# The small inverses and the layer norm of a hybrid attention block, issued step by step by the emission order

## The chip, the cores and the metric

One Trainium2 chip; the kernel runs on one of its cores. The metric is the device time of one execution in microseconds (us). Engines are named as in the profile: PE (TensorE's matmuls), PEld (its weight loads), DVE (VectorE), ACT (ScalarE), POOL (GpSimd), and SP (SyncE, which only issues DMAs here).

## The reference

One post-norm residual layer over x of 2048 tokens by 1024 channels, all float32. One wide projection of x feeds two token mixers: branch A, a gated delta rule with 4 heads of 128, and branch B, a sliding-window attention with a sink logit. Their outputs are gated, projected back to 1024 channels, merged, projected once more, and normalised. What the change touches is the triangular inverse inside the delta rule and the layer norm at the end:

```python
lower = jnp.where(strict, jnp.einsum("bnhid,bnhjd->bnhij", k_beta, k) * decay, 0.0)
t_inv = lax.linalg.triangular_solve(eye + lower, eye, left_side=True, lower=True, unit_diagonal=True)
...
r = DEEPNORM_ALPHA * x + out
mu = jnp.mean(r, axis=-1, keepdims=True)
var = jnp.mean(jnp.square(r - mu), axis=-1, keepdims=True)
y = (r - mu) * lax.rsqrt(var + LN_EPS) * ln_g + ln_b
```

## The kernel before

The 2048 tokens go in four chunks of T = 512. Every large product is made of three matmuls (high x high, high x low, low x high; lines 175 to 177), so PE has far more columns to stream than any other engine has elements. The order of PE's instructions is that of the program text (`manual_schedule` for PE). The other engines' and SP's instructions are put in order when the program is built, by a list scheduler that looks at when each is ready and, among ready ones, takes the one that was emitted first.

The text's own order comes from a small planner, `Order`. Its clock `st.now` counts PE time as the kernel's constants estimate it: 216 ns for a 512-column product (`PE_R`). "Dense" work (the large projections) is emitted piece by piece in the order of the string `ORDER`; after each piece `run` emits the next step of every task whose due time has come. A task is a generator that yields (PE time of the step, delay until its next step). `until(name)` polls every 500 ns until another task has ended; `finish(name)` moves the clock on until it has.

In chunks 1 to 3 the order begins

```python
ORDER = "kv k0 k1 q0 v0 p p p q1 p g w0 v1 z0 k2 q2 v2 g g g k3 z1 g q3 g w1 v3 g g g g z2 g g g z3 g g g"
```

`p` is a quarter of the output projection of the chunk before; after the fourth, `layer_norm` of that chunk is emitted in one go. `g` is a gate projection, `w0` the queries of the first half of the attention, which then spawns the task `attend` (window0).

Each of the 4 heads of a chunk passes through these tasks: `front` (k by k products at line 389, the matrix m2, its diagonal blocks of 32 to `scr_m` in DRAM and back as `su`), `inverse` (`small_inverse`: lines 905 to 917 on DVE, a chain of 16 pairs of a product, line 916, and a sum, line 917; then `xi` goes to `scr_p`, line 425), `levels` (loads it as `p_`, line 437; first matmuls at line 449), `back` (four rounds of PE line 496, DVE `bt` 498, PE 501, DVE `wc` 503, PE 507, DVE `S` 508) and `delta_gate`. `inverse` is spawned LAT_M = 4.4 us after its transfers are issued and emitted whole; `levels` and `back` are due LAT_INV = 29.6 us after the products of line 389, and `levels` yields LAT_D = 5.4 us between its loads and its first matmuls.

The layer norm before: for each of four blocks of 128 tokens, two bn_stats on DVE (line 699), the factors (line 685 to 691, with a power on POOL, line 851), and the normalising pass r*rs + nm on ACT (line 701); then for four quarters of the channels a load of gain and bias (`lg`, a buffer of the pool tag "s") and on POOL, in two halves each, a product (line 708) and a sum (line 709); then two output DMAs (line 712). The result lives in the buffers `yBh` and `yBl`, which `attend` of the same stretch overwrites from line 634 on.

Of the kernel before, what the change touches and what calls it, by code (L numbers as in the profile page):

```python
# [8 lines left out]
F32 = mybir.dt.float32  # L9
F32R = mybir.dt.float32r  # L10
AF = mybir.ActivationFunctionType
ALU = mybir.AluOpType
# [4 lines left out]
P = 128  # L17
# [3 lines left out]
NB = T // P  # L21
# [36 lines left out]
def view(t, off, dims):  # L58
    return bass.AP(tensor=t.tensor, offset=t.offset + off, ap=[list(t.ap[0])] + dims)


def build(tc, xt, xn, wk, wg, par, lnp, cst, out, seq=2048):
    nc = tc.nc
    NCH = seq // T
    with ExitStack() as ctx:
# [355 lines left out]
            yield 4 * PE_F, 0  # L421

        def inverse(h, su, xi):
            small_inverse(tc, pt.tile([P, 256], F32, name="xt"), su, xi.rearrange("p (c i) -> p c i", i=32))
            nc.sync.dma_start(out=at(scr_p[h % 2], 0, [[P, P], [1, P]]), in_=xi)
            yield 0, 0

        def levels(c, h, m2, q_):

            yield from st.until(f"front{h}")  # L430
            if h:
                yield from st.until(f"levels{h - 1}")
            p_ = pt.tile([P, NB, 64], F32, name="p_")
            nc.gpsimd.memset(p_[:32, :, 32:], 0.0)
            nc.gpsimd.memset(q_, 0.0)
            for i in range(4):
                nc.sync.dma_start(out=p_[32 * i:32 * i + 32, :, 32 * (i % 2):32 * (i % 2) + 32],
                                  in_=at(scr_p[h % 2], 1024 * i, [[32, 32], [4096, NB], [1, 32]]))
            yield 0, LAT_D
            for i in range(4):  # L440
                bi = slice(32 * i, 32 * i + 32)
                tc.keep_in_program_order(nc.vector.transpose(q_[bi, :, bi], p_[bi, :, 32 * (i % 2):32 * (i % 2) + 32]))
            copy = (lambda o, i: nc.scalar.activation(o, i, AF.Copy), nc.vector.tensor_copy)
            lo, hi = [slice(64 * s, 64 * s + 32) for s in range(2)], [slice(64 * s + 32, 64 * s + 64) for s in range(2)]
            x_ = pt.tile([P, NB, 64], F32, name="x_")
            ps = [p4(), pp.tile([P, NB, P], F32, name="pp")]
            for b in range(NB):
                for s in range(2):
                    nc.tensor.matmul(ps[s][hi[s], b, :32], m2[lo[s], b, hi[s]], p_[lo[s], b, :32], start=True, stop=True)
            for s in range(2):  # L450
                copy[s](x_[hi[s], :, :32], ps[s][hi[s], :, :32])
            yield 8 * PE_Q, LAT_B
            ps = [p4(), pp.tile([P, NB, P], F32, name="pp")]
            for b in range(NB):
                for s in range(2):
                    nc.tensor.matmul(ps[s][lo[s], b, :32], x_[hi[s], b, :32], q_[hi[s], b, hi[s]], start=True, stop=True)
            for b in range(NB):
                nc.tensor.matmul(ps[0][hi[0], b, :32], q_[hi[0], b, hi[0]], x_[hi[0], b, :32], start=True, stop=True)
            copy[0](p_[hi[0], :, :32], ps[0][hi[0], :, :32])
            for s in range(2):  # L460
                copy[1 - s](q_[lo[s], :, hi[s]], ps[s][lo[s], :, :32])
            yield 12 * PE_Q, LAT_B
            ps = p4()
            for b in range(NB):
                nc.tensor.matmul(ps[64:, b, :64], m2[:64, b, 64:], p_[:64, b], start=True, stop=True)
            copy[0](x_[64:], ps[64:, :, :64])
            yield 4 * PE_T, LAT_B
            ps = p4()
            for b in range(NB):
                nc.tensor.matmul(ps[:64, b, :64], x_[64:, b], q_[64:, b, 64:], start=True, stop=True)  # L470
            copy[1](q_[:64, :, 64:], ps[:64, :, :64])
            yield 4 * PE_T, LAT_B
# [100 lines left out]
        def attend(c, gp):  # L573
            for b0 in (0, 2):
                yield from st.until(f"qT{b0}")
            if not gp:
                c.yBh = py.tile([P, 4, T], F32R, name="yBh")
                c.yBl = py.tile([P, 4, T], F32R, name="yBl")
            zb = [c.z[f"zb{2 * gp + g}"] for g in range(2)]
# [100 lines left out]
            for bp in range(2):  # L680
                nc.vector.scalar_tensor_tensor(c.ra[bp][:, :, es], xr[bp], 2.0 * ALPHA, pss[bp], ALU.mult, ALU.add)

        def norm_factors(c, bst):
            mv = sm.tile([P, 2], F32, name="mv")
            nc.vector.bn_aggr(mv, bst)
            va = sm.tile([P, 1], F32, name="va")
            nc.vector.tensor_scalar(va, mv[:, 1:2], 4.0e-5, None, ALU.add)
            rs = sm.tile([P, 1], F32, name="rs")
            rsqrt(nc, sm, rs, va, mhalf)
            nm = sm.tile([P, 1], F32, name="lnm")  # L690
            nc.vector.scalar_tensor_tensor(nm, mv[:, 0:1], -1.0, rs, ALU.mult, ALU.mult)
            return rs, nm

        def layer_norm(c):
            for b in range(NB):
                r = c.ra[b // 2][:, b % 2]
                bst = sm.tile([P, 4, 6], F32, name="st", bufs=1)[:, :2]
                for i in range(2):
                    nc.vector.bn_stats(bst[:, i], r[:, 512 * i:512 * i + 512])
                rs, nm = norm_factors(c, bst)  # L700
                nc.scalar.activation(r, r, AF.Identity, scale=rs, bias=nm)
            for eg in range(4):
                es = slice(256 * eg, 256 * eg + 256)
                lg = pa.tile([P, 2, 256], F32, name="s")
                nc.sync.dma_start(out=lg, in_=bass.AP(tensor=lnp.tensor, offset=lnp.offset + 256 * eg, ap=[[0, P], [D, 2], [1, 256]]))
                for bp in range(2):
                    r = c.ra[bp][:, :, es]
                    nc.gpsimd.tensor_tensor(r, r, lg[:, 0:1].to_broadcast([P, 2, 256]), ALU.mult)
                    nc.gpsimd.tensor_tensor(r, r, lg[:, 1:2].to_broadcast([P, 2, 256]), ALU.add)
            for bp in range(2):  # L710
                t0 = c.i * T + bp * 256
                nc.sync.dma_start(out=out[t0:t0 + 256].rearrange("(b p) e -> p b e", p=P), in_=c.ra[bp])
# [47 lines left out]
        def piece(c, w):  # L760
            if w == "start":
                st.dense([start(c)])
            elif w == "kv":
                st.dense([window_kv(c)])
            elif w == "g":
                st.dense([gate(c, next(c.gates))])
            elif w == "p":
                e = next(c.projects)
                st.dense([project(c.prev, e)])
                if e == 3:  # L770
                    layer_norm(c.prev)
            elif w[0] == "w":
                st.dense([window_q(c, int(w[1]))])
            elif w[0] == "z":
                st.dense([silu2(c, f"h{w[1]}3")])
            else:
                st.dense([head_in(c, int(w[1]), w[0])])

        st = Order()
# [26 lines left out]
class Order:  # L806

    def __init__(self):  # L810
        self.now, self.tasks, self.done = 0.0, [], set()

# [4 lines left out]
    def step(self, t):  # L817
        try:
            dur, lat = next(t[2])
        except StopIteration:  # L820
            self.done.add(t[1])
            self.tasks.remove(t)
            return
        self.now += dur
        t[0] = self.now + lat
# [22 lines left out]
def rsqrt(nc, sm, r, a, mhalf):  # L848

    n = a.shape[1]  # L850
    nc.gpsimd.tensor_tensor(r, a, mhalf[:, :n], ALU.pow)
    t = sm.tile([P, n], F32, name=f"rsq{n}")
    nc.vector.tensor_tensor(t, r, r, ALU.mult)
    nc.vector.scalar_tensor_tensor(t, t, -0.5, a, ALU.mult, ALU.mult)
    nc.vector.scalar_tensor_tensor(r, t, 1.5, r, ALU.add, ALU.mult)
# [43 lines left out]
def small_inverse(tc, t, su, xi):  # L899


    rows = su.rearrange("p (m r k) -> p m r k", r=2, k=32)
    tm = t.rearrange("p (m k) -> p m k", k=32)
    nc = tc.nc
    tc.keep_in_program_order(nc.vector.memset(view(su, 33, [[66, 16]]), 0.0))
    for m in range(0, 16, 8):
        ms = slice(m, m + 8)
        nc.vector.tensor_tensor(tm, rows[:, ms, 1], view(su, 66 * m + 1, [[66, 8], [0, 32]]), ALU.mult)
        nc.vector.tensor_tensor(rows[:, ms, 0], rows[:, ms, 0], tm, ALU.add)
    nc.vector.memset(view(su, 0, [[33, 32]]), 1.0)  # L910
    tx = t.rearrange("p (c r k) -> p c r k", r=2, k=32)
    for i in range(30, -1, -2):
        n = 32 - i
        u = view(su, 33 * i, [[0, 4], [32, 2], [1, n]])
        x = view(xi, i, [[32, 4], [0, 2], [1, n]])
        nc.vector.tensor_tensor(tx[:, :, :, :n], u, x, ALU.mult)  # L916
        nc.vector.tensor_reduce(xi[:, :, i:i + 2], tx[:, :, :, :n], AX.X, ALU.add)  # L917


def tables(seq):  # L920
# [71 lines left out]
```

## Time and profile before

| | |
|---|---|
| median of 3 runs | 1720.17 us (1720.06 to 1723.12) |
| the profiled execution | 1723.25 us, span of its instructions 1721.5 us |
| PE busy | 1631.3 us, 95% of the span |
| DVE busy | 1020.2 us, 59% |
| ACT busy | 547.8 us, 32% |
| POOL busy | 374.2 us, 22% |
| mean granted TensorE clock | 0.983 |

Busy times of different engines overlap; only what keeps PE idle, or its clock low, can be won without taking work from PE.

### The profile page before, as it was taken

The page shows a single profiled execution, that of the slowest core. Times are in us where ns is not written, and L with a number is a line of the kernel's source. Part 1 is how long each engine was busy: PE and PEld are TensorE (multiplying, and loading weights), DVE is VectorE, ACT ScalarE, POOL GpSimd, SP SyncE. Part 2 cuts the span into 40 slices and gives each one's busy share as a digit, 9 for nine tenths or more (in the row PEclk, how much of TensorE's full clock was granted, in tenths as well). Part 3 has the DMA queues.
Part 4 walks back from the last instruction along what each step waited for, and adds up shares of the span by engine and source line. Part 5 has one row for each costly group of instructions (what it writes and reads, how often), then busy time and mean ns, then how long its engine had stood idle before and what let it go on. Part 6 is the DMA issues. An engine that isn't in the chain of part 4 may idle for free.

```text
span 1721.5 us, 27328 instructions
## 1 busy us (share of the span) xinstructions
PE 1631.3 (95%) x9846; PEld 1372.2 (80%) x9846; DVE 1020.2 (59%) x3118; ACT 547.8 (32%) x1496; POOL 374.2 (22%) x366
## 2 busy tenths in 40 slices
PE   8989999999897999999989899999998989999997
PEld 6867878778886878888888687888888868888787
DVE  5677678446757756435546765643554867463245
ACT  3454445333232532321303243323130334333100
POOL 4543454341334111010003311100010521100002
PEclk9999999999999999999999999999999999999999
DMA  8765675667685455557555645556656554464862
GB/s 301 241 219 193 209 245 190 216 204 237 204 251 186 130 168 167 142 165 240 176 167 172 205 133 159 159 152 191 190 167 213 176 168 142 145 189 141 279 204 80
DMA packets 189159, 323.39 MB, mean 188 GB/s; under 512 B 31072, under 2 KB 45408, under 8 KB 188896
## 3 DMA queue, kind: packets, MB, share of 16 engines
q1 hardware_dynamic: 185184, 316.40, 58.3%
q0 software_dynamic: 3840, 5.25, 1.4%
q8 instruction: 78, 1.28, 0.3%
q14 instruction: 57, 0.47, 0.1%
HBM read 244.97 MB, written 71.37 MB: 184 GB/s over the span
## 4 chain that ended last, share of the span: by engine, by line
PE 71%; DVE 13%; DMA 9%; issue 3%; ACT 2%; SPq 1%; POOL 1%; ACTq 0%; DVEq 0%; POOLq 0%
PE mm L175 19%; PE mm L177 18%; PE mm L176 18%; DVE xt L916 2%; DMA wb<-kw_o 2%; PE pp L627 2%; DVE kr L867 2%; PE pp L619 1%; DVE xi L917 1%; DMA w<-in_wg 1%; DMA su<-scrm 1%; DMA wb<-kw_kv 1%; PE pp L588 1%; PE pp L589 1%; PE pd L501 1%
## 5 line engine op out<-in xcount | busy, mean ns | idle before, releaser
L175 PE MATMUL mm<-xh,wb 128*128 128x512 f32 x1128 | 474.4, 421 | 0.9 <-DMA wb<-kw_h 0.9
L177 PE MATMUL mm<-xh,wb 128*128 128x512 f32 x1128 | 447.1, 396 | 0.0
L176 PE MATMUL mm<-xl,wb 128*128 128x512 f32 x1128 | 446.2, 396 | 0.0
L177 PEld LDWEIGHTS mm<-xh,wb 128*128 128x128 f32 x1128 | 213.5, 189 | 50.2
L175 PEld LDWEIGHTS mm<-xh,wb 128*128 128x128 f32 x1128 | 214.6, 190 | 44.6 <-issue 5.7
L176 PEld LDWEIGHTS mm<-xl,wb 128*128 128x128 f32 x1128 | 215.2, 191 | 35.6
L157 POOL TENSOR_TENSOR wb<-w,wb 128x512 fp32r<-128x512 f32 (+1 forms) x110 | 149.7, 1362 | 193.2 <-ACT wb L156 171.2
L175 PE MATMUL mm<-wb,s 128*128 128x256 f32 x384 | 113.2, 295 | 18.7 <-DMA wb<-kw_o 12.9
L175 PE MATMUL mm<-wb,xh 128*128 128x256 f32 (+1 forms) x384 | 115.1, 300 | 11.0 <-DVE rope L866 4.2
L176 PE MATMUL mm<-wb,s 128*128 128x256 f32 x384 | 109.9, 286 | 1.0 <-POOL wb L157 1.0
L176 PE MATMUL mm<-wb,xh 128*128 128x256 f32 (+1 forms) x384 | 110.1, 287 | 0.3 <-POOL wb L157 0.3
L177 PE MATMUL mm<-wb,s 128*128 128x256 f32 x384 | 109.7, 286 | 0.0
L177 PE MATMUL mm<-wb,xl 128*128 128x256 f32 (+1 forms) x384 | 109.6, 285 | 0.0
L156 ACT ACTIVATE wb<-w 128x512 fp32r<-128x512 f32 (+1 forms) x110 | 68.8, 629 | 115.8 <-PE mm L177 55.7
L916 DVE TENSOR_TENSOR xt<-su,xi 128x16 f32<-128x16 f32 (+15 forms) x256 | 99.4, 388 | 5.5
L175 PEld LDWEIGHTS mm<-wb,s 128*128 128x128 f32 x384 | 74.4, 194 | 22.9 <-DMA wb<-kw_o 15.4
L605 ACT ACTIVATE s<-s,nm 128x256 f32<-128x256 f32 (+1 forms) x128 | 62.7, 491 | 82.6 <-DVE nm L599 82.6
L175 PEld LDWEIGHTS mm<-wb,xh 128*128 128x128 f32 x384 | 74.0, 193 | 14.3 <-issue 6.3
L917 DVE TENSOR_REDUCE xi<-xt 128x8 f32<-128x16 f32 (+15 forms) x256 | 74.6, 291 | 5.9
L176 PEld LDWEIGHTS mm<-wb,s 128*128 128x128 f32 x384 | 74.3, 194 | 1.6 <-POOL wb L157 1.5
L176 PEld LDWEIGHTS mm<-wb,xh 128*128 128x128 f32 x384 | 74.0, 193 | 0.9 <-POOL wb L157 0.6
L177 PEld LDWEIGHTS mm<-wb,s 128*128 128x128 f32 x384 | 74.2, 193 | 0.0
(666 smaller groups left out, 3165.4 us busy)
## 6 DMA issues: line engine op xcount, KB each, us to landing
wb<-kw_h SPq DMA_DIRECT2D x96, 512.0 KB, 4.1
wb<-kw_g SPq DMA_DIRECT2D x96, 512.0 KB, 4.0
w<-in_wg SPq DMA_DIRECT2D x106, 256.0 KB, 4.1
wb<-kw_b SPq DMA_DIRECT2D x48, 512.0 KB, 4.6
wb<-kw_o SPq DMA_DIRECT2D x36, 512.0 KB, 4.9
kw_h<-wb SPq DMA_DIRECT2D x32, 512.0 KB, 3.9
kw_g<-wb SPq DMA_DIRECT2D x32, 512.0 KB, 3.4
wb<-kw_q SPq DMA_DIRECT2D x24, 512.0 KB, 4.0
```

The lines of the kernel that those rows point to most:

```text
L156: nc.scalar.activation(hi, raw, AF.Copy)
L157: nc.gpsimd.tensor_tensor(lo, raw, hi.bitcast(F32), ALU.subtract)
L175: nc.tensor.matmul(ps, sh, mh, start=(first and i == 0), stop=False)
L176: nc.tensor.matmul(ps, sh, ml, start=False, stop=False)
L177: nc.tensor.matmul(ps, sl, mh, start=False, stop=(last and i == n))
L501: nc.tensor.matmul(ps, q_[:, b], bt, start=True, stop=True)
L588: nc.tensor.matmul(psc[v][:, g, k0:], c.qT[v][:, b, g], kT[v][:, ks], start=True, stop=False)
L605: nc.scalar.activation(s[:, g, k0:], s[:, g, k0:], AF.Exp, bias=nm[:, g:g + 1], scale=0.125, accum_out=su[:, g:g + 1])
L627: nc.tensor.matmul(psY[64 * v:64 * v + 64], c.vs[b + kb][:, 64 * v:64 * v + 64], pTs[v][:, kb], start=(kb == kbs[0]), stop=(kb == 1))
L867: nc.vector.tensor_tensor(d[:, :, 0:8], a[:, 0, :, 0], a[:, 1, :, 1], ALU.subtract)
L916: nc.vector.tensor_tensor(tx[:, :, :, :n], u, x, ALU.mult)
L917: nc.vector.tensor_reduce(xi[:, :, i:i + 2], tx[:, :, :, :n], AX.X, ALU.add)
```

## The change

`inverse` and `layer_norm` become tasks that emit a step at a time. A step yields `None` in place of a PE time: the planner's clock then stands still and the task's own due time moves on. `small_inverse` yields after each of its two halves of row updates (1.8 us) and after each of its 16 pairs (420 + 40 n ns, n = 2 to 32 even). `layer_norm` is spawned after the fourth `p`; it yields 2.5 us after the factors of each of four blocks and 1.8 us after each of 16 steps. The normalising pass, the gain and the bias are now two DVE instructions for each 128 tokens by 256 channels: (r - mu) * gain, then r * rs + bias; ACT's pass and POOL's products and sums are gone. `levels` waits for the end of `inverse`, and `attend` of window0 for the end of `norm`. In `norm_factors`, `mv` and `rs` get four buffers.

```diff
         def inverse(h, su, xi):
-            small_inverse(tc, pt.tile([P, 256], F32, name="xt"), su, xi.rearrange("p (c i) -> p c i", i=32))
+            yield from small_inverse(tc, pt.tile([P, 256], F32, name="xt"), su, xi.rearrange("p (c i) -> p c i", i=32))
             nc.sync.dma_start(out=at(scr_p[h % 2], 0, [[P, P], [1, P]]), in_=xi)
-            yield 0, 0
+            yield None, 0
 
         def levels(c, h, m2, q_):
...
             if h:
                 yield from st.until(f"levels{h - 1}")
+            yield from st.until(f"inverse{h}")
...
             if not gp:
+                if c.i:
+                    yield from st.until("norm")
                 c.yBh = py.tile([P, 4, T], F32R, name="yBh")
...
-        def norm_factors(c, bst):
-            mv = sm.tile([P, 2], F32, name="mv")
+        def norm_factors(c, bst, bufs=None):
+            mv = sm.tile([P, 2], F32, name="mv", bufs=NB)
...
-            rs = sm.tile([P, 1], F32, name="rs")
+            rs = sm.tile([P, 1], F32, name="rs", bufs=NB)
             rsqrt(nc, sm, rs, va, mhalf)
+            if bufs:
+                return rs, mv[:, 0:1]
...
         def layer_norm(c):
+            fs = []
             for b in range(NB):
...
-                rs, nm = norm_factors(c, bst)
-                nc.scalar.activation(r, r, AF.Identity, scale=rs, bias=nm)
+                rs, mu = norm_factors(c, bst, NB)
+                fs.append((r, rs, mu))
+                yield None, 2500
             for eg in range(4):
...
-                for bp in range(2):
-                    r = c.ra[bp][:, :, es]
-                    nc.gpsimd.tensor_tensor(r, r, lg[:, 0:1].to_broadcast([P, 2, 256]), ALU.mult)
-                    nc.gpsimd.tensor_tensor(r, r, lg[:, 1:2].to_broadcast([P, 2, 256]), ALU.add)
+                for r, rs, mu in fs:
+                    nc.vector.scalar_tensor_tensor(r[:, es], r[:, es], mu, lg[:, 0], ALU.subtract, ALU.mult)
+                    nc.vector.scalar_tensor_tensor(r[:, es], r[:, es], rs, lg[:, 1], ALU.mult, ALU.add)
+                    yield None, 1800
...
                 if e == 3:
-                    layer_norm(c.prev)
+                    st.spawn("norm", layer_norm(c.prev), 0)
...
     def step(self, t):
...
+            return
+        if dur is None:
+            t[0] += lat
             return
...
 def small_inverse(tc, t, su, xi):
...
         nc.vector.tensor_tensor(rows[:, ms, 0], rows[:, ms, 0], tm, ALU.add)
+        yield None, 1800
...
         nc.vector.tensor_reduce(xi[:, :, i:i + 2], tx[:, :, :, :n], AX.X, ALU.add)
+        yield None, 420 + 40 * n
```

## Rows read from the trace of the kernel before

**Rows 1.** The page, part 1: busy us (share of the span) xinstructions of each engine.

```profile
PE 1631.3 (95%) x9846; PEld 1372.2 (80%) x9846; DVE 1020.2 (59%) x3118; ACT 547.8 (32%) x1496; POOL 374.2 (22%) x366
```

**Rows 2.** Windows: length, busy us of PE, PEld, DVE, ACT, POOL; PEclk; DMA.

```profile
500.00:560.00 60.00, 50.31 (x336) 42.80 (x333) 48.89 (x139) 15.68 (x41) 25.58 (x27) 0.97 0.63 193
920.00:980.00 60.00, 51.24 (x337) 44.28 (x337) 46.64 (x129) 13.91 (x32) 26.73 (x27) 0.91 0.61 189
1340.00:1400.00 60.00, 52.02 (x342) 45.30 (x341) 46.57 (x131) 14.72 (x36) 27.04 (x27) 0.91 0.61 191
...
1020.00:1080.00 60.00, 60.00 (x366) 48.70 (x365) 35.33 (x127) 22.35 (x70) 6.83 (x8) 1.00 0.52 154
```

**Rows 3.** Timeline of PE: start us, us, line, [idle before <-releaser].

```profile
542.46 0.80 PE L501 MATMUL pd<-bt,q__4948 128*128 128x128 f32 x2 [4.91 <-DVE bt L498]
...
964.39 0.58 PE L501 MATMUL pd<-bt,q__9191 128*128 128x128 f32 x1 [6.29 <-DVE bt L498]
...
1383.27 0.80 PE L501 MATMUL pd<-bt,q__13384 128*128 128x128 f32 x2 [6.18 <-DVE bt L498]
```

**Rows 4.** Timeline of DVE, 956 to 964 us.

```profile
956.10 6.99 DVE L867 TENSOR_TENSOR kr<-rope 128x32 f32<-128x32 f32 x1
...
963.99 0.35 DVE L498 SCALAR_TENSOR_TENSOR bt<-pd,neG,vt 128x128 f32<-128x128 f32 x1
```

**Rows 5.** Timeline of POOL, first and last of six instructions, 956 to 963 us.

```profile
956.27 1.30 POOL L708 TENSOR_TENSOR yBh<-yBh,s 128x512 f32<-128x512 f32 x1
...
961.77 1.26 POOL L709 TENSOR_TENSOR yBl<-yBl,s 128x512 f32<-128x512 f32 x1
```

**Rows 6.** Groups of DVE, 499 to 545 us: line, xcount | busy us, mean ns.

```profile
L867 DVE TENSOR_TENSOR kr<-rope 128x32 f32<-128x32 f32 x4 | 8.2, 2058 | 0.0
L916 DVE TENSOR_TENSOR xt<-su,xi 128x16 f32<-128x16 f32 (+15 forms) x16 | 7.2, 451 | 0.3
```

**Rows 7.** Groups of DVE, 1029 to 1047.3 us: an inverse away from layer norm.

```profile
L916 DVE TENSOR_TENSOR xt<-su,xi 128x16 f32<-128x16 f32 (+15 forms) x16 | 5.3, 330 | 0.3
```

**Rows 8.** Single lines over the span: count, duration ns min/median/max.

```profile
L867 DVE TENSOR_TENSOR kr<-rope x48: 145/182/6994, 41.2 to 1515.0; 128x32 f32<-128x32 f32 x32, 128x16 f32<-128x16 f32 x16
...
L909 DVE TENSOR_TENSOR su<-su,xt x32: 405/424/1410, 86.1 to 1513.3; 128x256 f32<-128x256 f32 x32
...
L318 DVE SCALAR_TENSOR_TENSOR k<-xs,par,k x48: 736/752/1714, 28.8 to 1467.8; 128x512 f32<-128x512 f32 x48
```

**Rows 9.** Timelines of SP, PE and DVE: inverses' ends, first matmuls of levels.

```profile
301.17 0.60 SPq L425 DMA_DIRECT2D scrp<-xi  x1
...
306.89 0.21 PE L449 MATMUL pp<-p__3496,m 32*32 32x32 f32 x1 [0.49 <-DMA p__3496<-scrp]
...
1029.70 0.07 DVE L905 MEMSET su<- 128x16 f32 x1 [1.40 <-DMA su<-scrm]
...
1046.74 0.35 SPq L425 DMA_DIRECT2D scrp<-xi  x1
...
1055.81 0.21 PE L449 MATMUL pd<-p__11011,m 32*32 32x32 f32 x1
...
1111.17 0.49 SPq L425 DMA_DIRECT2D scrp<-xi  x1
...
1118.27 0.21 PE L449 MATMUL pd<-p__11677,m 32*32 32x32 f32 x1
```

**Rows 10.** Timelines of PE and ACT, chunk 1; line 712's DMAs, issue to landing.

```profile
501.81 0.39 PE L175 MATMUL mm<-xh,wb 128*128 128x512 f32 x1
502.04 0.40 PE L176 MATMUL mm<-xl,wb 128*128 128x512 f32 x1
...
553.17 0.28 PE L588 MATMUL pp<-kT,qT 128*128 128x256 f32 x1
...
572.89 0.42 ACT L634 ACTIVATE yBh<-yb 128x256 fp32r<-128x256 f32 x1 [4.14 <-DVE yb L632]
...
DMA to landing us min/median/max: 6.1/8.3/9.5
```

## The prediction

> **What bounds the kernel now.** Read the page's busy times first: PE is busy for 95% of the span, DVE for 59%, POOL for 22% [rows 1]. So the kernel can gain only where PE is idle, or where its clock is low, and a faster DVE or POOL is worth nothing by itself. Next, the span in windows: away from the layer norm PE is busy for all of 60.00 us and DVE for 35.33 [rows 2]; in the three stretches that begin with the layer norm of the chunk before, PE is busy for 50.31, 51.24 and 52.02 of 60 us. That is 9.7 + 8.8 + 8.0 = 26.4 us of idle PE. The granted clock there is 0.97, 0.91 and 0.91 against 1.00, so PE also lost about 60 x (0.03 + 0.09 + 0.09) = 12.6 us at the lower of its two levels (1.2 in place of 2.4 GHz) while it was busy or waiting. These 39 us are what the change can win in this place.
>
> The timeline of PE tells what it waits for: one long wait in each stretch, 4.91, 6.29 and 6.18 us, together 17.4 of the 26.4, for `bt` of line 498 [rows 3]. The timeline of DVE tells why `bt` is late: a 32-column product of `rope`, line 867, which has a median of 182 ns, took 6.99 us, and `bt` ran right behind it [rows 4, 8]. The timeline of POOL tells what happened in that time: from 956.27 to 963.03 it ran without a break, five of its six instructions products and sums of the layer norm [rows 5]; line 867 ended as the last of them did. In the first stretch line 867 used 8.2 us in four instructions and the inverse's line 916 used 7.2 us in place of 5.3 [rows 6, 7]. So a run of POOL's elementwise work holds up those DVE instructions that read two SBUF operands, PE waits behind them, and its clock falls.
>
> **The change part by part.** *POOL's 16 products and sums of each layer norm go.* With them goes what held DVE up. The three long waits are 17.4 us. The other 9.0 us of idle PE are short waits for DVE in the same stretch, of which I credit half, 4.5. Of the 12.6 us of clock I credit two thirds, 8.4, as part of the small waits stays. Sum 30.3 us. The bounds are 0 and 39.
>
> The page "SBUF — State Buffer" of the Trainium skill, section "Who interferes with whom", says that a DVE instruction with two SBUF inputs and a GpSimd instruction that reads SBUF exclude each other, and that whoever is first has the port for the whole instruction. The trace agrees that they exclude each other but not on the length: line 867 lost 6.8 us, more than one POOL instruction of 1.30 [rows 4, 5]. What one instruction's hold would make of the time is the fourth rival.
>
> *DVE takes the work over.* For each of three chunks, 32 instructions of 128x256 are added. The trace has no such form; the nearest are a product of 128x256 from SBUF, 424 ns, and a scalar_tensor_tensor with a per-partition scalar over 128x512, 752 ns [rows 8], which cannot be longer at half the width. So 32 x 0.424 = 13.6 us is the lower end and 32 x 0.752 = 24.1 the upper one; I take 0.45, near the first because the columns are the same: 14.4 us. The first stretch had 48.9 us of DVE [rows 2]; take off 8.2 - 4 x 0.18 = 7.5 and 7.2 - 5.3 = 1.9 [rows 6 to 8], at least 9.4, and add 14.4: 53.9 us at most of DVE work beside some 50.3 of PE work. DVE would be all but full there. The work is spread: the layer norm has until its buffers are overwritten, and the windows behind have room (35.33 of 60). I charge 2 us in each stretch, 6 us; the bounds are 0 and 53.9 - 50.3 = 3.6 in each, 11.
>
> *The steps' place.* The new steps add no DMA and take none away; the loads of gain and bias, `xi`'s store and the two output DMAs leave later in SP's order. `attend` of window0 must wait for `norm`: 4 x 2.5 + 16 x 1.8 = 38.8 us of the planner after the last `p`. In the trace it starts 553.17 - 501.81 = 51.4 us after it, 41.7 without the idle time; a product that the planner counts as 216 ns takes 230 from start to start [rows 10], so 41.7 is 39.2 of the planner's. The wait ends just when the attention was due anyhow: nothing, up to one poll and one dense piece (0.5 + 1.3 us) in a chunk, hidden by the projections that PE has in hand; without that cover 3 x 1.8 = 5 us. Next late would be the overwriting of `yBh`: it came at 572.89 [rows 10], 563.2 without the idle time. The new layer norm ends by 501.8 + 38.8 x 1.065 + 5 (its queue on DVE) = 548, its output lands within 9.5 us, at 558. 5 us to spare, so nothing.
>
> *The inverse's steps.* Before, the whole chain had priority over all that was emitted after it; now work emitted between its steps goes first when both are ready. The planner ends the emission 8.0 + 21.2 = 29.2 us after the products of line 389 (0.9 + 2.7 + 4.4, then 2 x 1.8 + 17.6), and `levels` was due at 29.6: the new wait in the text costs nothing while `inverse` is not late by more than a poll. But the chip's DVE may end later. In the trace an inverse away from the layer norm took 1046.74 - 1029.70 = 17.0 us; if it now followed its emission to the end it would take 21.2 x 1.065 = 22.6, so it may slip by 0 to 5.6 us. From `xi`'s store to the first matmul of `levels` there were 9.1 us for the third head and 7.1 for the fourth, and 5.7 is what it needs: in chunk 0 PE was already waiting (0.49 us) with 5.7 [rows 9]. So 3.4 and 1.4 us are spare, and none in chunk 0. PE takes its instructions in order, so all the projections behind line 449 would wait. At a slip of 5.6 the cost is 2.2 + 2.2 + 4.2 (second head like the third) in each of three chunks and 3 x 5.6 in chunk 0: 42.6 us. I take a tenth, 4 us, since DVE has idle time outside the three stretches in which a chain of low priority still runs, and chunk 0's other work gains where the inverse no longer goes ahead of it.
>
> ACT's four passes per chunk go too; ACT is busy 32% [rows 1], so nothing. More buffers for `mv` and `rs` cost nothing.
>
> Sum: -30.3 + 6 + 4 = -20.3 us. The profiled execution took 1723.25 us, 1.75 more than its span of 1721.5 and 3.1 more than the median of the runs; the saving is taken from the median: 1720.2 - 20.3 = 1700 us.
>
> **The rivals.** *All of it:* no queue on DVE, no slip, clock back to 1.00: 1720.2 - 39 = 1681 us. For it: the clean windows show 60.00 of 60. Against it: DVE near full.
> *DVE becomes the bound of the stretches:* the long waits go, but the queue costs 11 us, the short waits all stay and half the clock: -17.4 - 6.3 + 11 + 4 = -8.7, 1711 us. For it: 53.9 us of work. Against it: part of it can wait.
> *The inverse ends too late* (slower): PE waits at line 449 in 12 heads. At the bound 1720.2 - 24.3 + 42.6 = 1738 us; it decides from an average wait of 2 us in the 12 heads. For it: no time to spare in chunk 0. Against it: DVE idle 25 of 60 us elsewhere.
> *The change does not do what it says:* POOL's run was not the cause of all of the 6.8 us, and only one instruction's hold, 3 x 1.3 = 3.9 us, goes, with half the short waits and a third of the clock: -3.9 - 4.5 - 4.2 + 10 = -2.6, 1718 us. Against it: the common end in rows 4 and 5.
>
> **How the numbers follow.** Forecast (about 1700, own range 1690 to 1708) 0.37; all of it 0.17; DVE the bound 0.23; inverse too late 0.15; no effect 0.08. A difference under 0.2% (3.4 us) can't be told from none. Faster: 0.37 + 0.17 + 0.23 = 0.77; same 0.08; slower 0.15. The range from 1681 to 1727 leaves out the far half of the slower case and little below.
>
> **What would show it.** Right: no POOL instruction of lines 708 and 709; line 867 never above some 2 us; no PE wait for line 498 over 2 us; PE busy for 55 us or more of the 60 behind the fourth `p`, clock 0.97 or better there; POOL's busy time near 312 us (374.2 less 48 instructions of 1.3), DVE's about the same as before. Wrong: waits at line 449 for `p_` that add up to over 10 us; waits for lines 498, 503 and 508 spread over the stretch; or SP waiting for line 712 with weights behind it.

## The result, and the profile after

The changed kernel takes 1738.1 us (median of 4 runs, 1735.9 to 1743.1) against 1721.2 (1720.1 to 1723.1) for the kernel before, measured on the same chip: a ratio of 1.0097, 95% interval 1.0080 to 1.0114. It is 1% slower; the forecast was 1700 us, and the range ended at 1727. The text has moved by some lines: lines 449, 498, 501, 503, 507, 867 and 916 of before are 450, 499, 502, 504, 508, 878 and 928 after, and the layer norm's new instructions are lines 714 and 715.

Part 1 of the page after, to be read beside [rows 1]:

```profile
PE 1639.6 (94%) x9846; PEld 1380.8 (79%) x9846; DVE 1024.2 (59%) x3202; ACT 533.9 (31%) x1484; POOL 315.4 (18%) x318
```

POOL has lost the 58.8 us that it was to lose, and DVE is as busy as before. The span went from 1721.5 to 1741.3 us, by 19.8. PE's busy time accounts for 8.3 of it (1631.3 to 1639.6 for the same 9846 instructions: more of them ran at the lower clock) and PE's idle time for the other 11.5. The mean granted clock of the whole span fell from 0.983 to 0.971.

The windows of after, the three stretches behind the fourth `p` and one away from the layer norm (columns as in [rows 2]):

```profile
500.00:560.00 60.00, 47.36 (x307) 41.61 (x307) 44.36 (x149) 8.69 (x24) 6.05 (x11) 0.91 0.65 197
922.00:982.00 60.00, 50.67 (x359) 44.67 (x359) 46.56 (x156) 10.61 (x33) 6.91 (x11) 0.92 0.63 196
1350.00:1410.00 60.00, 49.89 (x363) 44.11 (x361) 46.49 (x156) 10.75 (x34) 6.91 (x11) 0.94 0.64 195
1026.00:1086.00 60.00, 60.00 (x358) 47.88 (x356) 39.65 (x140) 24.63 (x74) 7.44 (x9) 1.00 0.52 152
```

The last row is as clean as it was. The stretches did not fill up: PE is busy for 47 to 51 us, no better than the 50 to 52 of before, though DVE has no more work in them than it had [rows 2]. What PE waits for there has changed. Its waits, by what ended them (us in total, times, longest):

```profile
PE pd L508 <- DVE wc L504: 12.6, 7, 3.8
...
PE pd L450 <- DMA p__5890<-scrp: 7.8, 1, 7.8
PE pd L450 <- DMA p__14284<-scrp: 7.2, 1, 7.2
PE pd L450 <- DMA p__10087<-scrp: 6.7, 1, 6.7
...
PE pd L502 <- DVE bt L499: 4.2, 7, 1.0
```

The long waits for `bt` [rows 3] are gone; none is over 1.0 us. In their place stand three waits at the first matmul of `levels`, 21.7 us in all, one in each of chunks 1 to 3, and waits for `wc`, which come to 12.6 us now, 3.3 to 3.8 in each of these chunks. Before, the same waits were

```profile
PE pd L507 <- DVE wc L503: 3.2, 7, 0.9
```

All three waits at line 450 belong to head 1, the head whose inverse falls into the layer norm's stretch. DVE's timeline shows that inverse in chunk 1 (the products that it starts from begin at 503.6 us; its first instruction is the memset of line 916, then lines 919 and 920, then sixteen pairs of 928 and 929, each of which needs the one before it):

```profile
519.06 0.87 DVE L714 SCALAR_TENSOR_TENSOR yBl<-yBl,mv,s 128x256 f32<-128x256 f32 x2
...
521.54 0.07 DVE L916 MEMSET su<- 128x16 f32 x1
...
526.12 0.19 DVE L928 TENSOR_TENSOR xt<-su,xi 128x32 f32<-128x32 f32 x1
528.66 0.88 DVE L714 SCALAR_TENSOR_TENSOR yBh<-yBh,mv,s 128x256 f32<-128x256 f32 x2 [2.35 <-DMA s<-in_lnp]
...
529.86 0.18 DVE L929 TENSOR_REDUCE xi<-xt 128x8 f32<-128x32 f32 x1
...
533.38 0.20 DVE L928 TENSOR_TENSOR xt<-su,xi 128x48 f32<-128x48 f32 x1
...
535.54 0.86 DVE L715 SCALAR_TENSOR_TENSOR yBl<-yBl,rs,s 128x256 f32<-128x256 f32 x2
...
536.59 0.18 DVE L929 TENSOR_REDUCE xi<-xt 128x8 f32<-128x48 f32 x1
...
551.15 0.42 DVE L929 TENSOR_REDUCE xi<-xt 128x8 f32<-128x256 f32 x1
```

Three links of the chain, at 526.12, 529.86 and 533.38, take 0.2 us each, and 3.7 and 3.5 us lie between their starts: the layer norm's instructions stand in the gaps, and the first of them holds the queue for 2.35 us more while it waits for its gain. PE's own timeline shows the two waits that follow from this in chunk 1, first for `wc`, then at line 450 for the inverse:

```profile
533.12 0.80 PE L508 MATMUL pd<-wc,ktl 128*128 128x128 f32 x2 [3.48 <-DVE wc L504]
...
555.94 0.31 PE L450 MATMUL pd<-p__5890,m 32*32 32x32 f32 x2 [7.81 <-DMA p__5890<-scrp]
```

The inverse lasts from 521.5 to 551.6 us, 30 us against 17.0 away from the layer norm [rows 9]. The inverses that stand elsewhere kept their length: head 2's in chunk 1 lasts 16.8 us, and lasted 16.9 before.

### The profile page after: what moved, and what is told of

It reads as the page before. It is cut to its first block, busy times and chain, and to the rows that moved or that the text cites. A ratio compares the mean times of both kernels' runs of the same rounds, so it can differ in the third digit from the quotient of the medians.

```text
span 1741.3 us, 27291 instructions
## 1 busy us (share of the span) xinstructions
PE 1639.6 (94%) x9846; PEld 1380.8 (79%) x9846; DVE 1024.2 (59%) x3202; ACT 533.9 (31%) x1484; POOL 315.4 (18%) x318
## 3 DMA queue, kind: packets, MB, share of 16 engines
q8 instruction: 78, 1.28, 0.3%
## 4 chain that ended last, share of the span: by engine, by line
PE 73%; DVE 11%; DMA 11%; issue 2%; ACT 1%; SPq 1%; POOL 1%; ACTq 0%; DVEq 0%; POOLq 0%
PE mm L175 20%; PE mm L177 19%; PE mm L176 19%; DMA wb<-kw_o 2%; DMA s<-in_lnp 2%; PE pp L630 2%; DVE xt L928 2%; PE pp L622 1%; DVE xi L929 1%; PE pd L508 1%; PE pp L591 1%; DMA scrp<-xi 1%; PE pd L389 1%; DMA wb<-kw_kv 1%; PE pp L592 1%
## 5 line engine op out<-in xcount | busy, mean ns | idle before, releaser
L177 PEld LDWEIGHTS mm<-xh,wb 128*128 128x128 f32 x1128 | 215.1, 191 | 51.2
L175 PE MATMUL mm<-wb,s 128*128 128x256 f32 x384 | 114.6, 298 | 18.2 <-DMA wb<-kw_o 12.3
L176 PE MATMUL mm<-wb,s 128*128 128x256 f32 x384 | 111.0, 289 | 1.4 <-POOL wb L157 1.4
L177 PE MATMUL mm<-wb,s 128*128 128x256 f32 x384 | 110.9, 289 | 0.0
L175 PEld LDWEIGHTS mm<-wb,s 128*128 128x128 f32 x384 | 75.8, 197 | 22.8 <-DMA wb<-kw_o 14.8
L928 DVE TENSOR_TENSOR xt<-su,xi 128x16 f32<-128x16 f32 (+15 forms) x256 | 89.4, 349 | 5.8
L176 PEld LDWEIGHTS mm<-wb,s 128*128 128x128 f32 x384 | 75.7, 197 | 2.1 <-POOL wb L157 1.9
L177 PEld LDWEIGHTS mm<-wb,s 128*128 128x128 f32 x384 | 75.4, 196 | 0.0
```

The lines of the kernel that those rows point to most:

```text
L175: nc.tensor.matmul(ps, sh, mh, start=(first and i == 0), stop=False)
L176: nc.tensor.matmul(ps, sh, ml, start=False, stop=False)
L177: nc.tensor.matmul(ps, sl, mh, start=False, stop=(last and i == n))
```

## The experiments

Four theories went into the first four runs. **A:** the layer norm's instructions go ahead of head 1's inverse on VectorE, PE reaches line 450 first, waits, and its clock falls. **B:** it is the late loads of gain and bias that hold VectorE's queue. **C:** the steps let all 16 inverses end later (the prediction's rival). **D:** it is the amount of work that VectorE was given, wherever it stands. Each ratio below is to the kernel before on the same chip, with its 95% interval.

**e1, the inverse emitted whole again.**

```diff
-            yield from small_inverse(tc, ...)
+            for _ in small_inverse(tc, ...):
+                pass
```

> The changed kernel, but the inverse is emitted whole again, as before; the layer norm keeps its steps on VectorE. Theory A (in the three stretches behind the fourth p, the layer norm's instructions go ahead of the second head's inverse on VectorE, and PE waits for it at the first matmuls of levels, 8.4, 7.6 and 7.9 us, with the clock falling behind it): those waits fall below 2 us each and the time to about 1710 us. Theory B (what costs is that the gain and bias land late and hold VectorE with the instructions queued behind): the waits for wc of line 504 stay at 3.5 us in each stretch and the time stays above 1725. Theory C (stepping makes all 16 inverses later): about 1720. Theory D (the amount of layer norm work on VectorE): 1738.

Measured: 1733.4 us, ratio 1.0060 (1.0041 to 1.0079). Theory A as it stood expected 1710 and missed. The inverse still lasted 30 us, and the waits at `levels` were still 7.1, 7.2 and 6.7 us: to be emitted earlier does not protect the chain. A reading that fits: the scheduler takes what it holds to be ready, the next link of a chain is not ready while the last one runs, and so an independent instruction takes the slot. The traces show the order that came of it and not the scheduler's estimates, and why as many as eight go into one gap stays open. This is theory A's second form, which the later runs test. The time is also 0.37% below the changed kernel's by the ratios, which no run explains.

**e2, only the inverse's steps.** The kernel before with the stepped inverse and the wait of `levels` for it; the layer norm stays with ScalarE and GpSimd.

```diff
-            small_inverse(tc, ...)
+            yield from small_inverse(tc, ...)
...
+            yield from st.until(f"inverse{h}")
```

> The kernel before with the inverse emitted in steps and levels waiting for it; the layer norm stays whole and on POOL. Theory C: about 1738 us, with waits at the first matmuls of levels in most heads. Theories A, B and D: within 5 us of the kernel before, 1716 to 1726, as an inverse away from the layer norm ends as early as before.

Measured: 1725.3 us, ratio 1.0009 (0.9993 to 1.0026). No difference that can be told from noise, and the waits for `bt` are still 17.1 us, against 19.5 in the kernel before: theory C falls.

**e3, the kernel before without GpSimd's products and sums.**

```diff
-                    nc.gpsimd.tensor_tensor(r, r, lg[:, 0:1]..., ALU.mult)
-                    nc.gpsimd.tensor_tensor(r, r, lg[:, 1:2]..., ALU.add)
+                    pass
```

> The kernel before without POOL's products and sums of the three layer norms (the gain and the bias of chunks 0 to 2 are left out). This measures the first term of the prediction, which credited 30.3 us with bounds of 0 and 39: right if the time is 1683 to 1700 us, line 867 is never above 2 us, and the three waits for bt are gone; if POOL's run was not the cause, it stays near 1720.

Measured: 1694.3 us, ratio 0.9831 (0.9814 to 0.9848). The stretches fill up (57.35, 57.20 and 60.00 of 60 us), and line 867, which had a maximum of 6994 ns [rows 8], no longer varies. The first and third stretch, and the durations of the line (ns, min/median/max):

```profile
500.00:560.00 60.00, 57.35 (x386) 48.80 (x386) 38.67 (x151) 20.23 (x52) 6.00 (x10) 1.00 0.70 210
...
1340.00:1400.00 60.00, 60.00 (x385) 50.89 (x385) 41.60 (x150) 21.11 (x57) 6.40 (x9) 0.99 0.63 183
```

```profile
L867 DVE TENSOR_TENSOR kr<-rope x48: 168/180/189, 40.8 to 1486.5; 128x32 f32<-128x32 f32 x32, 128x16 f32<-128x16 f32 x16
```

Head 1's inverse lasted 16.8 us in chunk 1 here. In the kernel before it had lasted 29.4 us, from 513.7 to 543.2 in chunk 1:

```profile
513.75 0.07 DVE L905 MEMSET su<- 128x16 f32 x1
...
542.77 0.42 DVE L917 TENSOR_REDUCE xi<-xt 128x8 f32<-128x256 f32 x1
```

So GpSimd's instructions had made it long; and yet no wait shows at line 449 there, with PE itself held for `bt` for 4.91 us in that stretch [rows 3].

**e4, gain and bias loaded early**, into the 16 buffers of another pool.

```diff
-                lg = pa.tile([P, 2, 256], F32, name="s")
+                lg = ps_.tile([P, 2, 256], F32, name="s")
```

> The changed kernel, but the four loads of gain and bias go to four of the sixteen buffers of the pool that the merged products have just left, so that all four can be issued at once and none waits for the layer norm's own progress. Theory B: VectorE's idle time for these loads (2.4 us at 528 us) and the waits for wc go, 3 x 3.5 us and part of the levels waits and of the clock: about 1720. Theory A: the layer norm gets ahead of the inverse all the more, the waits at levels stay near 7 us, and the time falls by less than 8 us, 1730 to 1738.

Measured: 1738.9 us, ratio 1.0089 (1.0061 to 1.0116), as after. The waits at `levels` shrank to 4.3 to 5.3 us, but the inverse now lasted 36 to 37 us and PE waited 6.3 us for `rope`: the wait moved, the time did not. The waits for `wc`, which theory B expected to go, stayed (12.2 us). VectorE's idle time for the loads only fell from 12.2 to 7.0 us, so the run does not take theory B's cause away altogether; less of it brought nothing, and e5 takes away nearly all of it.

**e5, the layer norm's pairs kept behind what was emitted before them.**

```diff
-                    nc.vector.scalar_tensor_tensor(r[:, es], ..., mu, ...)
+                    tc.keep_in_program_order(nc.vector.scalar_tensor_tensor(r[:, es], ..., mu, ...))
```

> After's kernel, but each pair of the layer norm's sums is kept on VectorE behind everything that was emitted before it, so that it can no longer go ahead of steps of head 1's inverse that were emitted earlier; the pairs still stand between the steps. Theory A in its second form (the inverse is a chain of 32 instructions that each wait for the last; any layer norm instruction that is ready takes the gap behind one of them, whatever the emission order says): the inverse of head 1 lasts between the 17 us of before and the 30 us of after, the waits at the first matmul of levels in head 1 of chunks 1 to 3 come to 2 to 6 us each instead of 7 to 8, time 1715 to 1732. Rival D (it is the amount of layer norm work on VectorE in the stretch, wherever it stands): within 0.3% of after, 1733 to 1743.

Measured: 1729.2 us, ratio 1.0027 (1.0009 to 1.0045). The time is in theory A's range, its reason is not: the inverse still lasted 30 us, since the pairs now stood between its steps by order instead of by readiness, and the waits at line 450 grew to over 9 us. What went are the long waits for `wc`, and with them nearly all of VectorE's idle time for the loads (0.5 us against 12.2). The inverse is as long without it, so theory B falls as the main cause. The three waits:

```profile
PE pd L450 <- DMA p__14284<-scrp: 9.9, 1, 9.9
PE pd L450 <- DMA p__10087<-scrp: 9.4, 1, 9.4
PE pd L450 <- DMA p__5890<-scrp: 9.4, 1, 9.4
```

**e6, the same work behind head 1's inverse.**

```diff
+            yield from st.until("inverse1")
             for eg in range(4):
...
-                    nc.vector.scalar_tensor_tensor(r[:, es], ..., mu, ...)
+                    tc.keep_in_program_order(nc.vector.scalar_tensor_tensor(r[:, es], ..., mu, ...))
...
-                    yield None, 1800
+                    yield None, 700
```

> After's kernel, but the layer norm's 32 long instructions of a chunk are emitted only when head 1's inverse has been emitted whole, are kept behind it on VectorE, and follow each other at 0.7 us instead of 1.8. The work and its engine are those of after. Theory A: head 1's inverse is back under 19 us, no wait over 2 us at the first matmul of levels in head 1, and the time comes near that of before without GpSimd's products and sums (1694): 1695 to 1712, faster than before. Rival D (the amount of layer norm work on VectorE): the waits only move to lines 499 to 509 behind the inverse, time 1725 to 1740. Rival E (attention waits for the norm's buffers): a wait of 5 us or more at the first matmuls of attend in chunks 1 to 3, time 1715 to 1730.

Measured: 1711.1 us, ratio 0.9912 (0.9887 to 0.9936). The inverse lasts 16.9 us, and no wait for it at line 450 is over 0.6 us: theory A's outcome. In chunk 1 it starts at 513.8 us, and this is its last sum:

```profile
530.23 0.42 DVE L930 TENSOR_REDUCE xi<-xt 128x8 f32<-128x256 f32 x1
```

Smaller waits came in its place, 3.6 to 4.7 us in each chunk, further on in `levels` (line 457, see e7). Against e3, which has none of this work, the same 32 instructions on the same engine cost 2.7% of the time in after's place and 0.8% in this one, so theory D falls. Attention's one long wait at its first matmuls (5.2 us, at 104 us) is in chunk 0, as it was before, and none came in chunks 1 to 3, so rival E falls too. The run changes three things at once: the place, the constraint on the order, and the pace of 0.7 us; e9 tells them apart.

**e7, e6 with the early loads of e4.**

```diff
-                lg = pa.tile([P, 2, 256], F32, name="s")
+                lg = ps_.tile([P, 2, 256], F32, name="s")
```

> The same, with the gain and bias loaded into buffers of the other pool, so that the loads need not wait for a free buffer. Theory A: within 0.3% of the kernel with the norm behind the inverse. Theory B (late loads of gain and bias hold VectorE): faster than that one by 0.4% or more.

Measured: 1705.4 us, ratio 0.9885 (0.9870 to 0.9901), 0.27% below e6 with intervals that overlap: within theory A's 0.3%, and no proof that the early loads are worth nothing here. With e10 it is the best version of the study, 1.2% below the kernel before and some 2% below the changed one. DVE's timeline in chunk 1 shows where the layer norm now stands:

```profile
530.75 0.42 DVE L930 TENSOR_REDUCE xi<-xt 128x8 f32<-128x256 f32 x1
...
533.29 0.47 DVE L715 SCALAR_TENSOR_TENSOR yBh<-yBh,mv,s 128x256 f32<-128x256 f32 x1
...
546.34 1.30 DVE L443 STREAM_TRANSPOSE q__5579<-p__5862 32x128 f32<-32x128 f32 x4
```

Here line 930 is the inverse's last sum and 715 the layer norm's first instruction. The transposes of line 443 belong to `levels` and stand behind most of the layer norm, and PE waits for them, 3.3 us in each chunk:

```profile
PE pd L457 <- DVE q__5579 L443: 3.3, 1, 3.3
PE pd L457 <- DVE q__9776 L443: 3.3, 1, 3.3
PE pd L457 <- DVE q__13973 L443: 3.3, 1, 3.3
```

**e8, the move alone:** the layer norm on VectorE, with it and the inverses emitted whole.

```diff
-                    st.spawn("norm", layer_norm(c.prev), 0)
+                    for _ in layer_norm(c.prev):
+                        pass
+                    st.done.add("norm")
```

> One part of the change alone: the layer norm goes to VectorE, but it and the inverses are emitted whole, as before, with no steps. Theory A: the gaps are taken all the same; head 1's inverse lasts 28 to 40 us, waits of 6 to 10 us at levels in head 1, time 1730 to 1745, within 0.5% of after. Rival (the steps are what costs, since they spread the layer norm over the inverse): faster than after by 0.8% or more, under 1724.

Measured: 1740.9 us, ratio 1.0092 (1.0070 to 1.0114), the same as the whole change, with an inverse of 34 to 37 us and waits of 6.7 to 6.8 at `levels`, as theory A expected. With e2 this divides the change: the inverse's steps alone make no difference, and the move alone makes all of it. (PE's other wait is for `S` here, 4.1 to 4.7 us in each chunk, and not for `wc`.)

**e9, the layer norm behind `levels` of head 1 as well**, to be rid of e7's three waits.

```diff
-            yield from st.until("inverse1")
+            yield from st.until("levels1")
```

> The kernel with the norm behind head 1's inverse and early gain loads (1705.4), but the layer norm's long instructions wait until head 1's levels have been emitted too. There the transposes at line 443 stood behind the layer norm, and TensorE waited 3.3 us for them once in each of chunks 1 to 3. Theory A (what costs is a chain of VectorE that TensorE waits for next, with independent work in its gaps): those three waits go, nothing replaces them, 1695 to 1704. Rival E (the layer norm's end now holds attention and its buffers): new waits of 3 us or more at lines 591 or 635 or for bt of head 1's chain, time 1705 to 1720.

Measured: 1734.5 us, ratio 1.0074 (1.0057 to 1.0090). A clear miss, on the slow side of both expectations. The three waits went, but the work now lies in the stretch in which head 2's products are made, and there PE waits for `ktl`, for attention's `s`, and at head 2's `levels`:

```profile
PE pd L378 <- DVE ktl L368: 9.0, 7, 2.2
PE pp L622 <- DVE s L614: 7.4, 3, 3.9
...
PE pd L450 <- DMA p__15122<-scrp: 4.1, 1, 4.1
...
PE pd L450 <- DMA p__6728<-scrp: 2.6, 1, 2.6
PE pd L450 <- DMA p__10925<-scrp: 2.5, 1, 2.5
```

These are 25.6 us, while e7's three waits of 3.3 went. Between the two profiled executions, 31.9 us apart, PE's idle time accounts for 19.0 and PE's longer busy time, for the same instructions at a lower granted clock (0.976 against 0.982), for 12.9. The constraint and the pace are those of e7, so neither is what won there; the place is. Late is not the same as out of the way.

**e10, the place of e7 for the layer norm of before:** the statistics kept behind head 1's inverse, then ScalarE and GpSimd, with e7's early loads.

```diff
+            yield from st.until("inverse1")
...
-                nc.vector.bn_stats(bst[:, i], r[:, ...])
+                tc.keep_in_program_order(nc.vector.bn_stats(bst[:, i], r[:, ...]))
```

> The same place, other engine: the layer norm of before (normalization on ScalarE, products and sums on GpSimd) with its first instructions, the statistics, kept behind head 1's inverse. Theory A, if the place is all: head 1's inverse under 19 us, long waits for bt gone from head 0's chain, time 1695 to 1710, as with VectorE in that place. Rival F (GpSimd's long instructions hold VectorE's wherever they stand): its products meet head 1's chain of bt, wc and S, with waits of 3 to 6 us there, time 1712 to 1730.

Measured: 1705.8 us, ratio 0.9897 (0.9877 to 0.9917). The same as with VectorE in that place, and 1% below the kernel before, though GpSimd does the work of before. e7's waits at line 457 are gone as well. Its first stretch:

```profile
500.00:560.00 60.00, 59.16 (x398) 50.84 (x397) 45.20 (x146) 17.55 (x47) 17.88 (x21) 1.00 0.65 194
```

GpSimd still holds VectorE: three instructions of line 318 took 5.23 us (0.75 each when alone [rows 8]). What PE waited for there was short: 1.3 us for the `wc` behind them. The cost now lies in the next windows (PE busy 56.1 us of 560 to 620), with a new wait of 2.6 us at attention's first matmuls in each of chunks 1 to 3.

**e11, after with the layer norm's second half left out.**

```diff
+                    if eg > 1:
+                        yield None, 1800
+                        continue
                     nc.vector.scalar_tensor_tensor(r[:, es], ..., mu, ...)
```

> After's kernel with half of the layer norm's long instructions left out (the second half of the features gets no product and no sum), the other half where after has it. Theory A: the half that is left, 16 instructions of some 0.46 us, still finds the first gaps of head 1's inverse or stands ahead of it; the inverse lasts 17 to 24 us, waits at levels of 0 to 5 us, time 1700 to 1720, between the kernel without products and sums (1694) and after (1738). Rival (a fixed cost of the steps or of the waits for norm and inverse): within 0.5% of after, over 1729.

Measured: 1720.2 us, ratio 0.9998 (0.9984 to 1.0012). Head 1's inverse lasted 22.5 to 24.4 us and the waits at line 450 were 4.5 to 4.7 us, with the time and the inverse at, or just over, the upper edge of what theory A expected. Between e3 and after the cost grows with the work that stands in the chain's way, by 1.7% for the first half and 1.0% for the second. The price is not a fixed one; that a part of the first 1.7% is fixed is not ruled out.

**e12, the layer norm behind head 1's inverse, shared by VectorE and GpSimd.** As in e10, the statistics wait for the inverse too.

```diff
+            yield from st.until("inverse1")
...
+                nc.scalar.activation(r[:, 512:], r[:, 512:], AF.Identity, scale=rs, bias=nm)
...
-            for eg in range(4):
+            for eg in (2, 0, 3, 1):
...
+                if eg > 1:
+                    for bp in range(2):
+                        nc.gpsimd.tensor_tensor(r, r, lg[:, 0:1]..., ALU.mult)
+                        nc.gpsimd.tensor_tensor(r, r, lg[:, 1:2]..., ALU.add)
+                    continue
```

> The layer norm behind head 1's inverse, shared: half of the features by VectorE's 16 long instructions, the other half by ScalarE and 8 of GpSimd's. With all of it on VectorE in this place the time was 1705.4, with all of it on GpSimd 1705.8. Theory A with the place as the cause: the stretch behind the inverse is taken for about half as long, so part of the 11 us that separate those two from the kernel without products and sums (1694.3) comes back, 1698 to 1705. Rival F (GpSimd's long instructions hold VectorE's, so that the two halves take as long together as one after the other): no gain, 1705 to 1712.

Measured: 1724.8 us, ratio 1.0010 (0.9997 to 1.0023). A miss: slower than with either engine alone. GpSimd's products ran just while VectorE had its half to do, in front of the transposes. GpSimd, then DVE, then PE in chunk 1 (lines 724 and 725 are VectorE's half, 874 a product of one column):

```profile
542.53 2.66 POOL L720 TENSOR_TENSOR yBh<-yBh,s 128x512 f32<-128x512 f32 x2
545.15 2.66 POOL L721 TENSOR_TENSOR yBh<-yBh,s 128x512 f32<-128x512 f32 x2
```

```profile
542.69 1.38 DVE L724 SCALAR_TENSOR_TENSOR yBh<-yBh,mv,s 128x256 f32<-128x256 f32 x1
544.00 1.21 DVE L874 TENSOR_TENSOR rsq<-rs 128x1 f32<-128x1 f32 x1
545.13 1.56 DVE L725 SCALAR_TENSOR_TENSOR yBh<-yBh,rs,s 128x256 f32<-128x256 f32 x1
546.62 1.21 DVE L875 SCALAR_TENSOR_TENSOR rsq<-rsq,va 128x1 f32<-128x1 f32 x1
...
549.99 1.30 DVE L443 STREAM_TRANSPOSE q__5540<-p__5810 32x128 f32<-32x128 f32 x4
```

```profile
550.76 0.28 PE L457 MATMUL pd<-q__5540,x__5951 32*32 32x32 f32 x2 [8.62 <-DVE q__5540 L443]
```

Four DVE instructions that take 0.47 or 0.15 us alone lost 4.1 us in all, right ahead of the transposes that PE waited 8.6 us for. That is most of what this wait grew by over e7's 3.3. The rest goes with the queue: statistics (1.28 us at 548.4) stand ahead of the transposes here, too. In e10, where GpSimd has all of the products, the transposes ran at 538.5 us, before the first of them.

## Why the prediction was wrong, by its own steps

*GpSimd's 16 products and sums go, 30.3 us.* Right, and well sized: e3 does this alone, 1.69% or 29 us, and it removes the long waits for `bt` by way of line 867. The parts fit as well: between the profiled executions PE's idle time fell by 19.2 us and its busy time by 9.5, where the step credited 21.9 of waits and 8.4 of clock.

*VectorE takes the work over, 6 us, bounds 0 and 11.* This is the step that failed. The duration was right (0.475 us against 0.45), and so was the total of DVE's busy time. But from e3, which has none of this work, to after lie 46 us by the ratios, some 15 in each stretch, where the step charged 2 and allowed 3.6. Between the two profiled executions (48.5 us apart) 30.7 of it is idle PE and 17.8 is PE busy for longer at a lower granted clock (0.971 against 0.988), for which the step had no term. It weighed the work against the room in the window, 53.9 us against 50.3, as if only a full engine could make PE late. DVE is idle in a fourth of the stretch, and PE waits all the same, because the work stands between the links of a chain that PE needs next. e6 and e7 show it: the same 32 instructions, some 20 us later, cost 14 and 9 us against e3, by the ratios, in place of 46. For such a place the step's upper bound was about right; e9 shows that not every later place is one.

*The inverse's steps, 4 us, a tenth of 42.6.* The steps cost nothing that can be measured (e2). Its premise, that a chain emitted whole has priority over what is emitted after it, is not borne out either: in e1 it was emitted whole and still lasted 30 us. The step looked at inverses away from the layer norm and at four heads with too little time to spare; it never asked what the layer norm does to the one inverse beside it. Its rival, the inverse that ends too late, named line 449, and its 1738 us is the time that came. That is a coincidence: it worked from 12 heads slipping by the steps, and 3 were late, by some 13 us each, by the layer norm. Its sign, over 10 us of waits at that line, did appear (21.7).

*Where the saving went.* 17.4 us of waits for `bt` became 21.7 at line 450 and 9.4 more for `wc`. Before the change, head 1's inverse was as long (29.4 us), but PE was held for `bt` before it reached line 449. With `bt` on time PE comes there earlier, while the inverse starts later. In chunk 1, counted from the products of line 389 (at 500.1 us before, 503.6 after), PE is at the line after 44.5 us where it took 51.2, and the inverse starts after 17.9 us where it took 13.6, and so ends after 47.9 where it took 43.1. Of before, the products and the first matmul at line 449, without a wait:

```profile
500.11 1.16 PE L389 MATMUL pd<-k 128*128 128x128 f32 x8
...
551.29 0.21 PE L449 MATMUL pd<-p__5900,m 32*32 32x32 f32 x1
```

PE's clock then falls in each stretch as it did before, to 0.91 to 0.94.

*The steps' place, 0.* Right: in chunks 1 to 3 attention's first matmuls show no wait for the norm's buffers. (Its one long wait, 4.7 us before and 5.0 after, is in chunk 0.)

*The signs.* Right: no GpSimd products, the line that was 867 at most 0.72 us, no wait for `bt` over 1.0, GpSimd at 315 us. Wrong: 55 us of PE in each stretch and a clock of 0.97.

*The hold of GpSimd on VectorE.* The page "SBUF — State Buffer" of the Trainium skill, section "SBUF: two separate sides", has the port that VectorE and GpSimd share locked for one whole instruction. e12 agrees: line 874 took 1.21 us, near one GpSimd instruction of 1.33, and ended with one. The 6.99 us of [rows 4] remain longer than that rule, and no run settled why.

What stays open: the 11 us between e7 and e3. The profiled executions split them into 5.2 us of idle PE and 5.9 of busy PE at a lower granted clock (0.982 against 0.988). The three waits of 3.3 us are the largest that e3 lacks, but no run removed them without adding others (e9, e10).

## What to carry to other kernels

Where a scheduler orders an engine's queue by readiness, a dependent chain of short instructions leaves gaps, and independent work goes into them; to emit the chain whole did not prevent it here. So before work is moved to an engine with idle time, find the chain there whose end another engine waits for next, and put the work behind that end (and ahead of the next chain). Place was worth 2% for VectorE (after against e7) and 1% for GpSimd (before against e10); the choice of engine was worth nothing in the good place, where e7 and e10 took the same time, and 1% in the bad one. When one wait goes, look what else was late in its shadow.

## What was not expected of the hardware

VectorE and GpSimd at once on the two halves of one job were slower (1724.8 us) than either alone (1705.4 and 1705.8). Part of it is the hold, as a one-column product on VectorE took 1.21 us beside GpSimd's products in place of 0.15; part is the work that stood ahead of the transposes, and no run separates the two.
